# First FFN of a two-layer diffusion backbone: sums of modulation vectors as trees of accumulating DMAs, and both halves of a column block swept together in two PSUM banks

## The chip, the cores and the metric

The kernel runs on one core of one Trainium2 chip. The metric is the time of one execution in microseconds (us) on the device. The engines are TensorE (PE; PEld is its weight load), VectorE (DVE), ScalarE (ACT), GpSimd (POOL) and SyncE (SP), which here only issues DMAs. Each engine works through its own queue in order.

## The reference

Two layers run over 256 latent tokens, and the first layer also over 256 context tokens, with a model width of 1024 and an FFN width of 2816. Every sub-layer is modulated by vectors that come from a conditioning vector:

```
m  = (silu(c)     @ ada_w[i] + ada_b[i])     # 9 vectors of 1024 for latent tokens
mc = (silu(c_ctx) @ ada_w[i] + ada_b[i])     # the same for context tokens
x  = half_step_ffn(x,   m[0], m[1], m[2],  ffn_w_in[i, 0], ffn_w_out[i, 0], ...)
ctx = half_step_ffn(ctx, mc[0], mc[1], mc[2], ...)          # first layer only
# mixer with m[3..5] (layer 0: neighbourhood attention; layer 1: short convolution)
# second FFN with m[6..8]
# h = x * (1 + scale) + shift
# FFN: (silu(h @ w_in[:, :2816]) * (h @ w_in[:, 2816:])) @ w_out
# update: layer_norm(alpha * x + w * gate * y)
```

The modulation vectors need no token, only `ada_w`: 9 x 1024 columns by 1024 rows for each layer, 37.7 MB each. The two vectors that the first FFN itself starts with (m[0], m[1] and mc[0], mc[1]) are made ahead of it; the vectors spoken of here are the later ones.

## The kernel before

**Precision.** Most matrix products are made of three matmuls: each operand is split into a high part (ScalarE, `activation` Copy into a reduced-precision type, line 216) and a low part (VectorE, subtraction, line 219), and high x high, low x high and high x low are added in PSUM. A *unit* of weights is a tile of 128 x 1024 with one raw, one high and one low buffer. Raw buffers number four, high and low buffers five each; in the first FFN one further high and low buffer (`ext[0] = 1`, tags whx and wlx) takes one unit in six.

**The first FFN** (from line 597, loops from line 778) handles 512 tokens together. Its 22 column blocks of 128 come in three parts of 8, 8 and 6. A block has two halves, the SiLU half and the factor half, each a PSUM bank of 128 x 512 that is summed over eight K chunks of 128 rows. Column blocks go in panels of mostly two, which share four weight units. For each block after the first panel the loop sweeps over K for the first half, then over K for the second. `f0_mm` issues the matmuls (line 729), `f0_gate` (lines 738, 739, 118, 119) makes SiLU on ScalarE, the product on VectorE and the split. After each part `out_gemm` multiplies by the part's rows of `w_out` in two column halves of four token tiles each (lines 170 to 173), and `residual` adds the result times the gate to x. The gates are loaded from a table in DRAM (line 793) after the first part's column blocks. After the third part each token tile is normalized: `finish_stats` computes rs with two instructions on POOL (lines 435, 436), VectorE normalizes x (line 446), and TensorE transposes the result (hT, line 454).

**The background.** `tick()` is called after every six matmuls and advances a generator, `stream`, at a rate of 0.45 steps per tick, later 0.44, and 0.6 from the third group on. It runs `ada(vecs)` for seven groups of two vectors. Groups one to three each make a latent and a context vector from the same eight loads (m = 2, 3, 4 of layer 0); groups four to seven make two latent vectors from sixteen loads (m = 5, 6; m = 7, 8; then m = 0, 1 and m = 2, 3 of layer 1). One step loads 128 rows of `ada_w` (tag ar, three buffers; line 316, SP queue) and lets VectorE multiply them by a column of silu(c) and add them to a sum tile of 128 x 1024 (tag acc, two buffers; the first product is line 305, the others line 307; two instructions per vector and step). After the last load the sum over the 128 partitions is left. It is made on TensorE: two matmuls per vector with a matrix of ones (line 342, eight instructions per group in the trace), VectorE adds the bias row (line 343), and SP stores the row into `scr`, the table of modulation vectors in DRAM (line 345). Three steps pass between. A group has 12 steps with eight loads and 20 with sixteen.

In a later stage (`on_pool[0]` true, second FFN of layer 0 and beyond) the same function leaves the partition sum to `sum_up`: POOL reduces over partitions (line 356) and adds the row to the table with an accumulating DMA (line 357). For that the table's part for layer 1, vectors 4 to 8, is set to the bias beforehand (line 1162).

**What sets the order.** TensorE's instructions stand in program order. Those of the other engines are ordered by a planner that takes what is ready by priority, program order being the default; `tc.high_priority` moves work up (the unit splits by 40 instructions, the evacuation of output banks by 60 and more), and the background's last groups down by 20. On each queue the order so found is then fixed.

Of the kernel before, what the change touches and what calls it, by code (L numbers as in the profile page):

```python
# [10 lines left out]
F32 = mybir.dt.float32  # L11
# [7 lines left out]
P = 128  # L19
D = 1024  # L20
# [55 lines left out]
def backbone_kernel(  # L76
# [21 lines left out]
    ext = [1, 0]  # L98
# [183 lines left out]
    bias_rows = []  # L282
# [4 lines left out]
    def ada(vecs):  # L287
# [4 lines left out]
        def accumulate(l, m, k, w):  # L292
            with ExitStack() as st:
                for i in gate_ins + (last_lo if on_pool[0] else []):
                    st.enter_context(tc.issue_after(i.ins))
                for i, vec in enumerate(vecs):
                    if vec[:2] != (l, m):
                        continue
                    if k == 0:
                        acc[i] = hp.tile([P, D], F32, tag="acc", bufs=2, name=nm("acc"))  # L300
                    sc = cst[:, k, vec[2]:vec[2] + 1]
                    for h in range(2):
                        src, a = (c[:, h * 512:(h + 1) * 512] for c in (w, acc[i]))
                        if k == 0:
                            nc.vector.tensor_scalar(a, src, sc, None, op0=ALU.mult)
                        else:
                            nc.vector.scalar_tensor_tensor(out=a, in0=src, scalar=sc, in1=a,  # L307
                                                           op0=ALU.mult, op1=ALU.add)
            if on_pool[0] and k == KC - 1:
                sums.extend((vec, acc[i]) for i, vec in enumerate(vecs) if vec[:2] == (l, m))  # L310

        loaded = []
        for l, m in dict.fromkeys((l, m) for l, m, _ in vecs):
            for k in range(KC):
                w = hp.tile([P, D], F32, tag="ar", bufs=3, name=nm("ar"))
                sync.dma_start(w, ada_w[l, k * P:(k + 1) * P, m * D:(m + 1) * D])
                loaded.append((l, m, k, w))
                if len(loaded) > (ADA_LAG if gate_ins else 0):
                    accumulate(*loaded.pop(0))
                yield 1  # L320
# [6 lines left out]
        n = 2 * len(vecs)  # L327
        if not bias_rows:
            bias_rows.append(hp.tile([P, 512], F32, tag="adab", name=nm("adab")))
            nc.gpsimd.memset(bias_rows[0], 0.0)  # L330
        bt = bias_rows[0]
        for i, (l, m, v) in enumerate(vecs):
            sync.dma_start(bt[64 * i:64 * i + 64:32], ada_b[l, m * D:(m + 1) * D].rearrange("(a b) -> a b", b=512))
        yield 1
        yield 1
        yield 1
        rows = hp.tile([P, 512], F32, tag="adar", name=nm("adar"))
# [5 lines left out]
        nc.vector.tensor_tensor(out=rows[:32 * n], in0=ps[:32 * n], in1=bt[:32 * n], op=ALU.add)  # L343
# [254 lines left out]
    ab0 = hp.tile([P, D], F32, tag="acc", bufs=2, name="ab0")  # L598
# [14 lines left out]
    def start_tile():  # L613
# [3 lines left out]
        return hp.tile([P, D], F32, tag="ar", bufs=3, name=nm("ar"))  # L617
# [133 lines left out]
    for q, (k0, n) in enumerate(steps):  # L751
# [11 lines left out]
        run(nxt)  # L763
    sync.dma_start(win_sb, win_mask)
# [397 lines left out]
    sync.dma_start(scr[1][0, 4 * D:9 * D].rearrange("(a b) -> a b", a=16), ada_b[1, 4 * D:9 * D].rearrange("(a b) -> a b", a=16))  # L1162
# [131 lines left out]
```

## Time and profile before

| | |
|---|---|
| median of 3 runs | 1246.97 us (1245.27 to 1247.7) |
| the profiled execution | 1245.72 us, its span 1243.9 us |
| granted TensorE clock | 0.998 |
| first FFN | from the start to about 397 us |
| DMA packets | 275.67 MB, mean 222 GB/s |

The span runs from the first to the last instruction of the profiled execution; what lies around it makes its time 1.8 us longer. A profile row of a group gives line, engine, operation, output <- inputs, shapes and count, then busy time and the mean of one in ns, then the idle time of that engine just ahead of the group and what ended it. In the rows of stretches each engine's busy us are followed by its number of instructions, and the last three numbers are the granted clock, the busy share of the 16 DMA engines and the rate. The duration of a matmul row (about 390 ns) is its passage through the array; matmuls overlap, so the distance of their starts tells what one costs.

### The profile page before, as it was taken

To read this page: it belongs to the slowest core of one execution; us is meant where nothing else is said; L and a number is where in the kernel's file an instruction comes from. 1 tells how busy PE (TensorE), PEld (TensorE's weight loads), DVE (VectorE), ACT (ScalarE), POOL (GpSimd) and SP (SyncE) were. 2 spreads that over 40 slices of the span, in tenths; PEclk is the share of its full clock that TensorE was granted. 3 is DMA by queue.
4 is the path that set the end of the run, shared out by engine and by line. 5 is a ranking of instruction groups with operands and counts; after the bars stand their busy time and mean duration, and the time that the engine had idled before them with its cause. 6 is when DMAs were issued, how large, how long until landed. Compare 5 with 4: busy or idle time off the path is not lost.

```text
span 1243.9 us, 17235 instructions
## 1 busy us (share of the span) xinstructions
PE 1227.4 (99%) x5794; PEld 996.5 (80%) x5794; DVE 962.4 (77%) x1675; ACT 645.3 (52%) x1233; POOL 83.7 (7%) x93
## 2 busy tenths in 40 slices
PE   8999999999999999999999999999999999999997
PEld 6787778778778878777788888888878887888886
DVE  3698997888778866888877677878767798877646
ACT  2433132321325556587777635678535644677631
POOL 0000000000001111120000020020020110000200
PEclk9999999999999999999999999999999999999999
DMA  9876578778852654554899857889966764899741
GB/s 317 289 248 224 186 237 286 268 254 283 279 189 70 187 112 89 122 110 139 262 300 304 275 195 251 233 272 321 282 199 227 234 207 152 231 293 265 249 154 68
DMA packets 232304, 275.67 MB, mean 222 GB/s; under 512 B 59622, under 2 KB 178910, under 8 KB 232216
## 3 DMA queue, kind: packets, MB, share of 16 engines
q1 hardware_dynamic: 232020, 274.54, 71.9%
q8 instruction: 45, 0.74, 0.2%
q14 instruction: 43, 0.35, 0.1%
q0 software_dynamic: 160, 0.02, 0.0%
q10 hardware_dynamic: 36, 0.02, 0.0%
HBM read 265.27 MB, written 2.20 MB: 215 GB/s over the span
## 4 chain that ended last, share of the span: by engine, by line
PE 90%; DVE 5%; ACT 3%; DMA 1%; issue 1%; POOL 0%; SPq 0%; DVEq 0%; ACTq 0%
PE f L729 19%; PE w L170 17%; PE w L171 17%; PE w L173 17%; PE wkv L170 2%; PE wkv L171 2%; PE wkv L173 2%; PE wc L170 2%; PE wc L173 2%; PE wc L171 2%; PE ada L658 1%; PE S L1024 1%; PE hT L454 1%; DVE w1l L219 1%; PE wq L170 1%
## 5 line engine op out<-in xcount | busy, mean ns | idle before, releaser
L219 DVE TENSOR_TENSOR w1l<-w1r,w1h 128x512 fp32r<-128x512 f32 (+1 forms) x352 | 229.7, 697 | 44.0 <-ACT w1h L216 43.0
L216 ACT ACTIVATE w1h<-w1r 128x512 fp32r<-128x512 f32 (+1 forms) x352 | 198.7, 618 | 114.7 <-DMA w1r<-in_ffn_w_in_dram 38.3
L170 PE MATMUL w<-w1h,hTh 128*128 128x512 f32 x528 | 206.3, 391 | 1.2 <-ACT hTh L118 1.2
L171 PE MATMUL w<-w1l,hTh 128*128 128x512 f32 x528 | 205.6, 389 | 0.0
L307 DVE SCALAR_TENSOR_TENSOR acc<-ar,cst,acc 128x512 f32<-128x512 f32 x266 | 186.7, 749 | 14.4 <-DMA ar<-in_ada_w_dram 13.8
L170 PE MATMUL w<-w2h,gh 128*128 128x512 f32 (+1 forms) x446 | 173.3, 389 | 0.0
L171 PE MATMUL w<-w2l,gh 128*128 128x512 f32 (+1 forms) x446 | 172.3, 387 | 0.8 <-DVE w2l L219 0.8
L216 ACT ACTIVATE w2h<-w2r 128x512 fp32r<-128x512 f32 x176 | 101.5, 624 | 136.8 <-PE w L173 104.8
L173 PE MATMUL w<-w1h,hTl 128*128 128x512 f32 x528 | 162.7, 389 | 0.0
L219 DVE TENSOR_TENSOR w2l<-w2r,w2h 128x512 fp32r<-128x512 f32 x176 | 114.0, 688 | 56.0 <-ACT w2h L216 54.6
L173 PE MATMUL w<-w2h,gl 128*128 128x512 f32 (+1 forms) x446 | 136.1, 386 | 0.0
L729 PE MATMUL f<-h0h,w1h 128*128 128x512 f32 x352 | 133.8, 396 | 0.4 <-DVE h0h L684 0.4
L729 PE MATMUL f<-h0l,w1h 128*128 128x512 f32 x352 | 133.2, 391 | 0.0
L729 PE MATMUL f<-h0h,w1l 128*128 128x512 f32 x352 | 132.8, 390 | 0.0
L170 PEld LDWEIGHTS w<-w1h,hTh 128*128 128x128 f32 x528 | 99.1, 188 | 22.5 <-ACT hTh L118 2.1
L173 PEld LDWEIGHTS w<-w1h,hTl 128*128 128x128 f32 x528 | 99.0, 188 | 21.0 <-DVE hTl L119 0.4
L171 PEld LDWEIGHTS w<-w1l,hTh 128*128 128x128 f32 x528 | 99.1, 188 | 20.6 <-DVE w1l L219 0.3
L170 PEld LDWEIGHTS w<-w2h,gh 128*128 128x128 f32 x446 | 83.8, 188 | 19.2 <-issue 1.7
L171 PEld LDWEIGHTS w<-w2l,gh 128*128 128x128 f32 x446 | 83.8, 188 | 18.1 <-DVE w2l L219 1.7
L173 PEld LDWEIGHTS w<-w2h,gl 128*128 128x128 f32 x446 | 83.3, 188 | 17.1
L729 PEld LDWEIGHTS f<-h0h,w1h 128*128 128x128 f32 x352 | 66.3, 190 | 18.9 <-issue 4.2
L729 PEld LDWEIGHTS f<-h0l,w1h 128*128 128x128 f32 x352 | 65.5, 188 | 14.4 <-issue 0.6
(197 smaller groups left out, 1769.9 us busy)
## 6 DMA issues: line engine op xcount, KB each, us to landing
w1r<-in_ffn_w_in_dram SPq DMA_DIRECT2D x340, 256.0 KB
ar<-in_ada_w_dram SPq DMA_DIRECT2D x128, 512.0 KB
w2r<-in_ffn_w_out_dram SPq DMA_DIRECT2D x88, 512.0 KB
ar<-in_ada_w_dram SPq DMA_DIRECT2D x32, 256.0 KB
wkvr<-in_na_w_qkv_dram SPq DMA_DIRECT2D x32, 256.0 KB
wcr<-in_sc_w_in_dram SPq DMA_DIRECT2D x32, 256.0 KB
wqr<-in_na_w_qkv_dram SPq DMA_DIRECT2D x8, 512.0 KB
wor<-in_na_w_out_dram SPq DMA_DIRECT2D x8, 512.0 KB
```

What stands on the lines that cost most here:

```text
L170: nc.tensor.matmul(ps, lh, rh, start=first and i == 0, stop=False)
L171: nc.tensor.matmul(ps, lh, rl, start=False, stop=False)
L173: nc.tensor.matmul(ps, ll, rh, start=False, stop=last and i == n - 1)
L216: last_split[:] = [nc.scalar.activation(hi[:, a:a + m // W_HI], raw[:, a:a + m // W_HI], AF.Copy)]
L219: last_lo[:] = [nc.vector.tensor_tensor(out=lo[:, a:b], in0=raw[:, a:b], in1=hi[:, a:b].bitcast(F32), op=ALU.subtract)]
L307: nc.vector.scalar_tensor_tensor(out=a, in0=src, scalar=sc, in1=a, op0=ALU.mult, op1=ALU.add)
L454: nc.tensor.transpose(ps[:, k * P:(k + 1) * P], z[h][:, k * P:(k + 1) * P], ident)
L658: nc.tensor.matmul(ps[o:o + 32, 0:m], cst[:, a * kt + i, :], w[:, i, j, :], start=(a == 0 and i < 2), stop=(a == last and i >= kt - 2))
L729: nc.tensor.matmul(ps, w, hT0[k][part == 1], start=(k == part == 0), stop=(k == KC - 1 and part == 1))
L1024: nc.tensor.matmul(banks[i], (qh, qh, ql)[f][ps, qs], (kh, kl, kh)[f][ps, :], start=f == 0, stop=f == 2)
```

## The change

- In groups two to seven the partition sum is no longer on TensorE. When a vector's last product is issued, POOL's queue gets seven DMAs, each of which adds the upper half of the remaining rows of the sum tile to the lower half on chip (64 rows, 32, ... 1), and an eighth that adds the one row left to the table in DRAM. Each waits for the one before it. Two vectors that are ready together alternate.
- The first group is still summed on TensorE, without the bias; VectorE copies the result, and POOL adds it to the table.
- The bias is put into the whole of the table by three DMAs on SP at the beginning of the first FFN's main loop; the loads of bias rows and the later initialization go away.
- In the first FFN, sums have four buffers for two, and ada loads four for three; VectorE's products always run one step behind the load. The extra high and low weight buffer goes away. A group has 11 steps with eight loads and 19 with sixteen.
- Both banks of a column block are opened together, and one sweep over K alternates between them every six matmuls.

```diff
-    ext = [1, 0]
+    ext = [0, 0]
...
-    bias_rows = []
...
                     if k == 0:
-                        acc[i] = hp.tile([P, D], F32, tag="acc", bufs=2, name=nm("acc"))
+                        acc[i] = hp.tile([P, D], F32, tag="acc", bufs=2 if on_pool[0] else 4, name=nm("acc"))
...
-            if on_pool[0] and k == KC - 1:
-                sums.extend((vec, acc[i]) for i, vec in enumerate(vecs) if vec[:2] == (l, m))
+            if k == KC - 1:
+                ready = [(vec, acc[i]) for i, vec in enumerate(vecs) if vec[:2] == (l, m)]
+                if on_pool[0]:
+                    sums.extend(ready)
+                elif made[0]:
+                    n = P // 2
+                    while n:
+                        for _, a in ready:
+                            nc.gpsimd.dma_start(a[0:n], a[n:2 * n], accum_op=ALU.add)
+                        n //= 2
+                    for (l, m, v), a in ready:
+                        nc.gpsimd.dma_start(scr[l][v:v + 1, m * D:(m + 1) * D], a[0:1], accum_op=ALU.add)
...
-                w = hp.tile([P, D], F32, tag="ar", bufs=3, name=nm("ar"))
+                w = hp.tile([P, D], F32, tag="ar", bufs=3 if on_pool[0] else 4, name=nm("ar"))
...
-                if len(loaded) > (ADA_LAG if gate_ins else 0):
+                if len(loaded) > ADA_LAG:
                     accumulate(*loaded.pop(0))
...
-        for i, (l, m, v) in enumerate(vecs):
-            sync.dma_start(bt[64 * i:64 * i + 64:32], ada_b[l, m * D:(m + 1) * D].rearrange("(a b) -> a b", b=512))
-        yield 1
-        yield 1
-        yield 1
-        rows = hp.tile([P, 512], F32, tag="adar", name=nm("adar"))
+        for _ in range(3 if made[0] else 2):
+            yield 1
+        if made[0]:
+            return
+        rows = sp.tile([P, 512], F32, tag="s2", bufs=S2, name=nm("adar"))
...
-        nc.vector.tensor_tensor(out=rows[:32 * n], in0=ps[:32 * n], in1=bt[:32 * n], op=ALU.add)
+        nc.vector.tensor_copy(rows, ps)
         for i, (l, m, v) in enumerate(vecs):
-            sync.dma_start(scr[l][v, m * D:(m + 1) * D].rearrange("(a b) -> a b", b=512),
-                           rows[64 * i:64 * i + 64:32, :])
+            nc.gpsimd.dma_start(scr[l][v, m * D:(m + 1) * D].rearrange("(a b) -> a b", b=512),
+                                rows[64 * i:64 * i + 64:32, :], accum_op=ALU.add)
...
+    for l, v, r in ((0, 0, slice(2 * D, 9 * D)), (0, 1, slice(2 * D, 5 * D)), (1, 0, slice(0, 9 * D))):
+        sync.dma_start(scr[l][v, r].rearrange("(a b) -> a b", a=16), ada_b[l, r].rearrange("(a b) -> a b", a=16))
     sync.dma_start(win_sb, win_mask)
...
-                    bk = []
-                    for z in range(2):
-                        bk.append(mmb("f0", z))
-                        for k in range(0, KC, 2):
+                    bk = [mmb("f0", z) for z in range(2)]
+                    for k in range(0, KC, 2):
+                        for z in range(2):
                             f0_mm(bk[z], p, units, j, z, (k, k + 1))
                             tick()
...
-    sync.dma_start(scr[1][0, 4 * D:9 * D].rearrange("(a b) -> a b", a=16), ada_b[1, 4 * D:9 * D].rearrange("(a b) -> a b", a=16))
```

More of the change, by code (lines that the diff above doesn't have):

```diff
@@ L326, in ada @@
             return
[L327 to L331, printed above, removed]
-        for i, (l, m, v) in enumerate(vecs):
-            sync.dma_start(bt[64 * i:64 * i + 64:32], ada_b[l, m * D:(m + 1) * D].rearrange("(a b) -> a b", b=512))
-        yield 1
-        yield 1
-        yield 1
-        rows = hp.tile([P, 512], F32, tag="adar", name=nm("adar"))
+        for _ in range(3 if made[0] else 2):
[3 more added lines that the diff above has]
+        rows = sp.tile([P, 512], F32, tag="s2", bufs=S2, name=nm("adar"))
         ps = tpb("ada")
@@ L597, in backbone_kernel @@
     w_in, w_out = ffn_w_in[0, 0], ffn_w_out[0, 0]
-    ab0 = hp.tile([P, D], F32, tag="acc", bufs=2, name="ab0")
+    ab0 = hp.tile([P, D], F32, tag="acc", bufs=2 if on_pool[0] else 4, name="ab0")
     nc.vector.memset(ab0, 0.0)
@@ L616, in start_tile @@
             return hp.tile([P, 2, 512], F32, tag="pt", bufs=4, name=nm("ar")).rearrange("p a b -> p (a b)")
-        return hp.tile([P, D], F32, tag="ar", bufs=3, name=nm("ar"))
+        return hp.tile([P, D], F32, tag="ar", bufs=4, name=nm("ar"))
     marks = []
```

## The prediction

> **What bounds the kernel now.** I read the page first, then the busy time by stretches, then the chain of waits in order of time, then the timelines of single engines.
>
> ```profile
> PE 1227.4 (99%) x5794; PEld 996.5 (80%) x5794; DVE 962.4 (77%) x1675; ACT 645.3 (52%) x1233; POOL 83.7 (7%) x93
> ```
>
> ```profile
> core 0: us, PE busy (x) PEld busy (x) DVE busy (x) ACT busy (x) POOL busy (x), PEclk, DMA share, GB/s
> 97.00:135.00 38.00, 38.00 (x174) 30.48 (x170) 35.06 (x57) 10.59 (x19) 0.00 (x0) 1.00 0.65 222
> 135.00:173.00 38.00, 38.00 (x174) 30.49 (x170) 36.73 (x60) 9.20 (x16) 0.00 (x0) 1.00 0.63 200
> ...
> 268.00:314.00 46.00, 46.00 (x210) 37.24 (x206) 39.20 (x63) 12.11 (x22) 0.00 (x0) 1.00 0.80 265
> 314.00:361.00 47.00, 47.00 (x212) 38.21 (x204) 38.20 (x61) 15.86 (x28) 0.00 (x0) 1.00 0.74 246
> ```
>
> TensorE has the whole of these stretches of the first FFN, at a granted clock of 1.00. So time leaves this stage only with work that leaves TensorE, and every wait that reaches TensorE is added in full. VectorE comes next: 35.1 and 36.7 of 38 us while the second and third group of sums run. POOL does nothing here, so what is put on it has the engine to itself until the LayerNorm at the stage's end.
>
> The part that the change removes from TensorE shows in the chain of waits, once for each of the seven groups:
>
> ```profile
> 96.85 1.00 PE ada L342 x8
> ...
> 134.80 1.00 PE ada L342 x8
> ...
> 172.75 0.99 PE ada L342 x8
> ...
> 221.57 1.00 PE ada L342 x8
> ...
> 267.68 0.99 PE ada L342 x8
> ...
> 313.79 1.00 PE ada L342 x8
> ...
> 361.25 1.00 PE ada L342 x8
> ```
>
> **What leaves TensorE.** The timeline of PE around the first of them gives the price:
>
> ```profile
> 96.24 0.39 PE L729 MATMUL f<-h0h,w1l 128*128 128x512 f32 x1
> 96.47 0.39 PE L729 MATMUL f<-h0l,w1h 128*128 128x512 f32 x1
> 96.78 1.06 PE L342 MATMUL ada<-acc,ones 128*32 128x512 f32 x8
> 97.78 0.50 PE L729 MATMUL f<-h0h,w1h 128*128 128x512 f32 x1
> 98.12 0.39 PE L729 MATMUL f<-h0h,w1l 128*128 128x512 f32 x1
> ```
>
> Ordinary matmuls start 0.227 us apart (96.24 to 96.47 is 0.23). From 96.47 to 98.12 two periods should pass, 0.45 us; 1.65 pass. One group costs TensorE 1.20 us: the chain's 1.00 and 0.2 of switching around it. Six groups of seven go to DMAs: 6 x 1.20 = 7.2 us. The first stays as it is.
>
> **The two-bank sweep.** It issues the same matmuls, so TensorE gains nothing by itself. What it moves is when a weight buffer comes free. One unit is two pieces on ACT and two on VectorE:
>
> ```profile
> L216 ACT ACTIVATE w2h<-w2r 128x512 fp32r<-128x512 f32 x176 | 101.5, 624 | 136.8 <-PE w L173 104.8 <-DMA w1r<-in_ffn_w_in_dram 15.5 <-DMA w2r<-in_ffn_w_out_dram 8.1
> L219 DVE TENSOR_TENSOR w2l<-w2r,w2h 128x512 fp32r<-128x512 f32 x176 | 114.0, 688 | 56.0 <-ACT w2h L216 54.6
> ```
>
> That is 2 x 0.624 + 2 x 0.688 = 2.6 us. A panel of two column blocks holds four units; the ring had five and one extra buffer, and loses the extra one. Before, the third unit of the next panel takes the buffer that the last sweep frees 18 matmuls before its end, and is needed 12 matmuls into the next: 30 x 0.227 = 6.8 us. Now the second unit takes the one freed 36 matmuls before the end and is needed 12 in: 48 x 0.227 = 10.9 us. So with one buffer less the column blocks are safer than before. The output matmuls keep their order and only lose the buffer: between their two column halves the second unit has 18 + 6 matmuls, 5.4 us, for 2.6 us of work. With VectorE as full as above this can reach TensorE. Bounds: nothing, or the whole 2.6 us at each of three places, 7.8 us; I take 0.5, since 2.8 us are left over. SiLU now finds its bank done six matmuls (1.4 us) before the other instead of 24. The last gate is needed 12 to 18 matmuls after the last sweep: I take nothing, at most 0.4 us three times.
>
> **VectorE.** Rows of its groups in 97 to 173 us:
>
> ```profile
> L307 DVE SCALAR_TENSOR_TENSOR acc<-ar,cst,acc 128x512 f32<-128x512 f32 x56 | 38.6, 751 | 0.0
> L305 DVE TENSOR_SCALAR acc<-ar,cst 128x512 f32<-128x512 f32 x8 | 3.5, 481 | 2.9 <-PE ada L342 2.9
> L343 DVE TENSOR_TENSOR adar<-ada,adab 128x512 f32<-128x512 f32 x2 | 1.4, 684 | 0.0
> ```
>
> A later group takes fewer background steps, 11 for 12 and 19 for 20, so the same sums come faster. Groups two and three had 24 steps in 76 us; 22 take (76 - 2.4) x 22/24 = 67.5. VectorE's 71.8 us are 42.1 of sums, 1.4 of L343 and 28.3 that go with the matmuls, which become 25.1. 42.1 + 25.1 = 67.2 of 67.5: full. Its waits for L342 go, and with a lag of one step and a fourth buffer also those for the loads. A backlog would be worked off in the fourth group, where the rate falls. Between 0 and 3 us on TensorE; I take 0.5.
>
> **POOL and the trees.** Each vector becomes seven halvings and one DMA into the table in DRAM, eight DMAs that must wait for each other, all on POOL's queue. The trace has no halving. Nearest are the DMAs that POOL already accumulates with, and one small load into on-chip memory:
>
> ```profile
> L357 POOL DMA_DIRECT2D scr<-red x5: 997/997/1118, 727.2 to 1156.2; - x5
> ...
> DMA to landing us min/median/max: 2.7/3.4/4.9
> ```
>
> ```profile
> 1.37 2.21 DMA crow<-in_c_ctx_dram
> ```
>
> ```profile
> L255 ACTq DMA_DIRECT2D crow<-in_c_ctx_dram x1: 289/289/289, 1.4 to 1.4; - x1
> ```
>
> The small load needs 2.21 - 0.29 = 1.9 us after its issue; behind POOL's 1.0 that makes 2.9. A halving lies between 2.7 and 3.4 us; I take 2.8, by the lower end, because it ends on chip as that load does and the first FFN has the DMA engines 0.63 to 0.80 busy. The halvings also move 127 rows of 4 KB, 0.52 MB; at the 380 GB/s of the row below, 1.4 us if nothing overlaps. A tree: 7 x 2.8 + 3.4 + 1.4 = 24.4 us; with the ends, 7 x 2.7 + 2.7 + 0 = 21.6 to 8 x 3.4 + 1.4 = 28.6.
>
> ```profile
> 60.00:65.00 5.00, 5.00 (x24) 4.14 (x23) 5.00 (x9) 2.14 (x5) 0.00 (x0) 1.00 1.07 380
> ```
>
> How often do trees come? Groups two and three make two at once, 33.6 us apart: these fit. From the fourth on each group makes two, one after each eight loads, in 19 steps of (361.25 - 172.75)/80 = 2.36 less the 1.2 saved per group, about 2.3: 43.7 us, one tree per 21.9. At 24.4 they fall behind, 2.5 us each. The first of these eight is ready at about 182 us (group four starts at 173, 9.5 us earlier by three saved steps and 2.4 by TensorE, and needs nine steps). Four sum buffers let a sum start while three older trees are still at work, so VectorE isn't held up. But POOL's queue is in order, and behind the trees stands the LayerNorm:
>
> ```profile
> 385.71 0.19 POOL L435 TENSOR_TENSOR rs<-mv,lnc 128x1 f32<-128x1 f32 x1 [381.47 <-DVE mv L433]
> 385.98 0.57 POOL L436 TENSOR_TENSOR rs<-rs,lnc 128x1 f32<-128x1 f32 x1
> ```
>
> ```profile
> 388.58 0.87 PE hT L454 x8
> ```
>
> rs is wanted at 385.7 - 7.2 = 378.5, and the transposes on TensorE follow 2.9 us after it, with the normalizing of x in between and no slack that I can see. POOL is free when the eighth tree has issued its last DMA, 2.4 us before the tree ends: 182 + 8T - 2.4 <= 378.5 gives T <= 24.9 us. My 24.4 fits, barely. Each us of T above it costs TensorE 8 us.
>
> One rule of the skill speaks against putting this on POOL. The VectorE products of L305 take 481 ns where L307 takes 751 for the same shape, so they run in a faster mode; two of them fall in each tree. The Trainium skill, SBUF — State Buffer, section "SBUF: two separate sides", says that while VectorE runs an instruction in a two-port mode GpSimd cannot write the descriptors of its DMAs. By that rule a tree could grow by up to 2 x 0.48 = 1.0 us and the end by 8; as L305 has 1.0 of every 21.9 us, 0.1 per tree is likelier, and no run yet shows it. The same skill, DMA: Bandwidth & Descriptors, section "Anatomy of one DMA — SWDGE (gpsimd) path", gives 2.0 us per DMA plus bytes at 436 GB/s: a tree of 17.2 us, an estimate by that page, with nothing late. The rows above say more per DMA, and I go by them.
>
> **The rest.** Twenty-eight small DMAs leave SP's queue (fourteen bias rows, fourteen stores) and three initializing ones join it ahead of the mask, rope and ada loads; TensorE waited for none of them: nothing. The one of the later stage moves here. The first group's store goes over POOL and lands 3.4 us after its issue; the gate load waits for it on SP with ada and w2 loads behind it. One saved step (38.0/12 = 3.2 us) covers nearly all of that, and the residual that reads the gate comes after the whole first quarter of the output matmuls: nothing. The trees read twice and write once, 12 x 0.52 x 3 = 18.7 MB over 270 us, 69 GB/s beside 265: below the 380 seen, so nothing (bound 2 us).
>
> **Sum.** 7.2 - 0.5 - 0.5 = 6.2 us. The profiled execution took 1245.7 us (span 1243.9): 1239.5. It lies 1.3 below the median of 1247.0, from which the sum gives 1240.8. I forecast 1240.0.
>
> **Rivals.** *POOL falls behind (slower).* The place is rs L435 behind the eighth tree; it decides from T = 24.9 us, 2.9 us a halving. For it: the median landing of 3.4, and T within 0.5 us of the limit by my own count. Against it: those landings end in DRAM. At 28.6 us rs is 30 us late, 1239.5 + 30 = 1269; in the middle, 26.7, 15 us late, 1254. *The gain is eaten.* VectorE is full in groups two and three and the output matmuls lose their spare buffer: 3 us of backlog and 2 to 4 of refills leave 1243 to 1246. For it: 67.2 of 67.5. Against it: the load waits on VectorE end, and the sweeps relieve it.
>
> **How the numbers follow.** Forecast 0.60, by itself 1237 to 1243. POOL behind 0.27, eaten 0.13. A measurement of this kernel can tell 0.2%, 2.5 us, from no change. Faster: 0.60, the part of the second with T up to 25.4 (0.03) and the mildest of the third (0.04): 0.67. Same: 0.09 of the third and 0.02 of the second, 0.11. Slower 0.22. The range begins at 1237, the forecast without its two stalls (1239) less the 2 us by which runs of this kernel differ, and ends at 1257, T = 27; about 0.1 lies above, 0.05 below.
>
> **What would show it.** No L342 after the first; starts of TensorE 0.227 us apart through the stage, transposes hT at about 382. POOL's DMAs: the gap from one halving to the next should be 2.7 to 3.0 us. If rs stands behind a DMA of the last tree, or VectorE waits on a sum buffer, T was too small in my count. If w L171 waits on w2l at the middle of an output matmul, the buffer was missed.

## The result: slower by 2.1 %, and the profile after

The changed kernel takes 1273.32 us (median of four, 1273.07 to 1273.72) beside 1247.05 (1245.27 to 1247.7) for the one before: a ratio of 1.0213, 95 % interval 1.0201 to 1.0225. The forecast was 1240.0, its range ended at 1257. The profiled execution took 1273.07 us, its span is 1271.0 (before 1243.9).

The page of the changed kernel: the span, engines, DMA queues and chain.

```profile
span 1271.0 us, 17247 instructions
...
PE 1232.7 (97%) x5746; PEld 1001.0 (79%) x5746; DVE 959.2 (75%) x1669; ACT 643.7 (51%) x1233; POOL 161.1 (13%) x190
...
q0 software_dynamic: 4064, 6.33, 3.4%
...
PE 65%; DMA 15%; DVE 9%; issue 5%; ACT 3%; POOL 2%; SPq 0%; DVEq 0%; POOLq 0%; ACTq 0%
```

TensorE issues 48 matmuls fewer (5746 for 5794), as meant. POOL's queue moves 4064 packets, and DMAs hold 15 % of the chain that ended last. The same kernel in stretches of the first FFN's middle:

```profile
core 0: us, PE busy (x) PEld busy (x) DVE busy (x) ACT busy (x) POOL busy (x), PEclk, DMA share, GB/s
97.00:135.00 38.00, 38.00 (x169) 31.48 (x168) 38.00 (x62) 10.46 (x19) 6.20 (x8) 1.00 0.86 268
...
200.00:250.00 50.00, 47.12 (x200) 38.08 (x199) 39.23 (x63) 12.91 (x24) 12.89 (x16) 0.97 0.97 323
250.00:300.00 50.00, 42.65 (x164) 32.42 (x163) 44.09 (x70) 10.51 (x19) 11.62 (x14) 0.90 0.95 293
...
314.00:361.00 47.00, 45.84 (x190) 37.73 (x191) 28.05 (x45) 13.71 (x24) 14.62 (x19) 0.93 0.65 178
```

TensorE no longer has the whole of the stage: it is idle for 2.9 and 7.4 of 50 us, and the granted clock falls to 0.90 there. The DMA engines, 0.80 busy before, are 0.95 to 0.97 busy from 200 to 300 us, and 0.65 busy after 314 (before 0.74). So the background's products ran *earlier* than before, not later: the last starts at 330.1 us, before at 352.2.

Where the 27.1 us of span come from shows in the starts of rs on POOL. The first is at 403.76 (before 385.71, forecast 378.5): 18.0 us are lost up to that point, and the forecast's gain with them. 3.9 more are lost up to the second layer norm (609.10 for 587.19), 0.8 from there to the last rs and 4.4 after it. From 97 to 350 us TensorE is idle for 13.9 us; much of the rest of the loss is matmuls that start further apart, as the rows below show.

POOL's timeline at the end of the trees, and the landings of its DMAs (output <- input, size, median us from issue to landing):

```profile
386.79 0.78 POOL L319 DMA_DIRECT2D scr<-acc  x1 [1.68 <-DMA acc<-acc]
403.76 0.19 POOL L438 TENSOR_TENSOR rs<-mv,lnc 128x1 f32<-128x1 f32 x1 [16.19 <-DVE mv L436]
```

```profile
acc<-acc POOLq DMA_DIRECT2D x12, 256.0 KB, 7.0
acc<-acc POOLq DMA_DIRECT2D x12, 128.0 KB, 5.8
acc<-acc POOLq DMA_DIRECT2D x12, 64.0 KB, 4.6
acc<-acc POOLq DMA_DIRECT2D x12, 32.0 KB, 4.9
acc<-acc POOLq DMA_DIRECT2D x12, 16.0 KB, 4.0
acc<-acc POOLq DMA_DIRECT2D x12, 8.0 KB, 4.2
acc<-acc POOLq DMA_DIRECT2D x12, 4.0 KB, 4.6
scr<-acc POOLq DMA_DIRECT2D x12, 4.0 KB, 3.3
```

The landings of a tree add up to 38.4 us, where 24.4 were forecast. Yet the place that the slower rival named isn't where it hurts: ahead of rs POOL was idle for 16.19 us and waited for VectorE's mv. The loss reaches TensorE by another way, which two of the stalls show. ScalarE, VectorE and TensorE of the changed kernel, around 206 us:

```profile
192.47 0.58 ACT L741 ACTIVATE sil<-f 128x512 f32<-128x512 f32 x1
204.96 0.64 ACT L118 ACTIVATE gh<-sil 128x512 fp32r<-128x512 f32 x1 [11.91 <-DVE sil L742]
205.50 3.21 ACT L216 ACTIVATE w1h<-w1r 128x512 fp32r<-128x512 f32 x6
```

```profile
196.59 1.41 DVE L306 SCALAR_TENSOR_TENSOR acc<-ar,cst,acc 128x512 f32<-128x512 f32 x2 [2.23 <-DMA ar<-in_ada_w_dram]
199.09 1.41 DVE L306 SCALAR_TENSOR_TENSOR acc<-ar,cst,acc 128x512 f32<-128x512 f32 x2 [1.08 <-DMA ar<-in_ada_w_dram]
201.22 1.42 DVE L306 SCALAR_TENSOR_TENSOR acc<-ar,cst,acc 128x512 f32<-128x512 f32 x2 [0.71 <-DMA ar<-in_ada_w_dram]
...
204.24 0.68 DVE L742 TENSOR_TENSOR sil<-sil,f 128x512 f32<-128x512 f32 x1
...
208.20 1.29 DVE L219 TENSOR_TENSOR w1l<-w1r,w1h 128x512 fp32r<-128x512 f32 x2
```

```profile
206.16 0.50 PE L732 MATMUL f<-h0h,w1h 128*128 128x512 f32 x1
208.94 0.80 PE L732 MATMUL f<-h0h,w1l 128*128 128x512 f32 x1 [2.28 <-DVE w1l L219]
209.53 0.63 PE L732 MATMUL f<-h0l,w1h 128*128 128x512 f32 x1
209.96 0.63 PE L732 MATMUL f<-h0h,w1h 128*128 128x512 f32 x1
210.39 0.63 PE L732 MATMUL f<-h0h,w1l 128*128 128x512 f32 x1
```

Read it backwards. TensorE waits 2.28 us for w1l. VectorE makes w1l late because ScalarE made w1h late (six splits stand at 205.50 behind gh), and because more products of the background stand ahead of w1l. gh waits 11.91 us for the gate's product L742, though SiLU was done at 193.05. L742 stands in VectorE's queue behind the background's products, which wait 4.0 us for ada loads that are late and take most of the other time themselves. Behind the stall the matmuls start 0.43 us apart for a while instead of 0.23. The largest group of stalls, 6.4 us in four waits at the second output matmul (253 to 267 us), came the same way: there L742 stood behind 6.8 us of late loads, and gh waited 13.22 us for it.

The second stall shows a held sum buffer. VectorE and TensorE around 312 us:

```profile
309.77 0.88 DVE L304 TENSOR_SCALAR acc<-ar,cst 128x512 f32<-128x512 f32 x2 [2.89 <-DMA scr<-acc]
310.57 2.07 DVE L306 SCALAR_TENSOR_TENSOR acc<-ar,cst,acc 128x512 f32<-128x512 f32 x3
...
314.42 1.29 DVE L219 TENSOR_TENSOR w1l<-w1r,w1h 128x512 fp32r<-128x512 f32 x2
```

```profile
315.16 0.79 PE L732 MATMUL f<-h0h,w1l 128*128 128x512 f32 x1 [3.26 <-DVE w1l L219]
```

ScalarE had made the high parts by 310.2. VectorE stood 2.89 us until a tree's last DMA had landed, did products and residuals that stand ahead in its queue, and made the low part 3.26 us too late.

VectorE's waits in the background's products over the whole kernel, changed and then before; they all lie between 97 and 380 us:

```profile
L306 DVE SCALAR_TENSOR_TENSOR acc<-ar,cst,acc 128x512 f32<-128x512 f32 x266 | 186.2, 741 | 31.5 <-DMA ar<-in_ada_w_dram 31.2
...
L307 DVE SCALAR_TENSOR_TENSOR acc<-ar,cst,acc 128x512 f32<-128x512 f32 x266 | 186.7, 749 | 14.4 <-DMA ar<-in_ada_w_dram 13.8
```

So VectorE's waits for ada loads in these products add up to 31.2 us (before 13.8), those for a sum buffer to 4.6, and gh waits 75.4 us for the product between 97 and 380 us (before 53.6).

### The profile page after: what moved, and what is told of

Same layout as the page of the kernel before. It is cut to its first block, busy times and chain, and to the rows that moved or that the text cites. A ratio compares the mean times of both kernels' runs of the same rounds, so it can differ in the third digit from the quotient of the medians.

```text
span 1271.0 us, 17247 instructions
## 1 busy us (share of the span) xinstructions
PE 1232.7 (97%) x5746; PEld 1001.0 (79%) x5746; DVE 959.2 (75%) x1669; ACT 643.7 (51%) x1233; POOL 161.1 (13%) x190
## 3 DMA queue, kind: packets, MB, share of 16 engines
q0 software_dynamic: 4064, 6.33, 3.4%
## 4 chain that ended last, share of the span: by engine, by line
PE 65%; DMA 15%; DVE 9%; issue 5%; ACT 3%; POOL 2%; SPq 0%; DVEq 0%; POOLq 0%; ACTq 0%
PE w L171 14%; PE w L170 14%; PE w L173 14%; DMA acc<-acc 12%; PE f L732 7%; PE wkv L170 2%; PE wkv L171 2%; PE wkv L173 2%; PE wc L170 2%; PE wc L173 2%; PE wc L171 2%; DMA ar<-in_ada_w_dram 1%; DVE acc L306 1%; DVE w1l L219 1%; ACT pr L1036 1%
## 5 line engine op out<-in xcount | busy, mean ns | idle before, releaser
L219 DVE TENSOR_TENSOR w1l<-w1r,w1h 128x512 fp32r<-128x512 f32 (+1 forms) x352 | 231.0, 699 | 41.1 <-ACT w1h L216 39.2
L306 DVE SCALAR_TENSOR_TENSOR acc<-ar,cst,acc 128x512 f32<-128x512 f32 x266 | 186.2, 741 | 31.5 <-DMA ar<-in_ada_w_dram 31.2
L171 PE MATMUL w<-w1l,hTh 128*128 128x512 f32 x528 | 205.6, 389 | 0.0
L171 PE MATMUL w<-w2l,gh 128*128 128x512 f32 (+1 forms) x446 | 174.8, 393 | 3.3 <-DVE w2l L219 3.2
L170 PEld LDWEIGHTS w<-w1h,hTh 128*128 128x128 f32 x528 | 99.2, 188 | 22.6 <-ACT hTh L118 2.1
L171 PEld LDWEIGHTS w<-w1l,hTh 128*128 128x128 f32 x528 | 99.2, 188 | 20.3
L171 PEld LDWEIGHTS w<-w2l,gh 128*128 128x128 f32 x446 | 84.8, 190 | 23.6 <-DVE w2l L219 7.1
L316 POOL DMA_DIRECT2D acc<-acc x84 | 68.5, 858 | 201.1 <-DMA acc<-acc 180.4
L732 PEld LDWEIGHTS f<-h0h,w1l 128*128 128x128 f32 x352 | 66.9, 191 | 21.9 <-DVE w1l L219 8.1
```

Source lines behind the costliest of these rows:

```text
L170: nc.tensor.matmul(ps, lh, rh, start=first and i == 0, stop=False)
L171: nc.tensor.matmul(ps, lh, rl, start=False, stop=False)
L219: last_lo[:] = [nc.vector.tensor_tensor(out=lo[:, a:b], in0=raw[:, a:b], in1=hi[:, a:b].bitcast(F32), op=ALU.subtract)]
L316: nc.gpsimd.dma_start(a[0:n], a[n:2 * n], accum_op=ALU.add)
L732: nc.tensor.matmul(ps, w, hT0[k][part == 1], start=(k == part == 0), stop=(k == KC - 1 and part == 1))
```

## The experiments

Each measured time is a median, and in brackets stands the ratio to the kernel before, run beside it, with its 95 % interval. In the expectations of no_halvings, thin_halvings and sweep_no_extra, A is the theory that the halvings cost the time (A1 by their bytes, A2 by the long chain that holds the sum buffers), and B that the lost weight buffer, the joint sweep or the faster steps do.

### What the halvings cost, and by what

**no_halvings.** The halvings are left out.

```diff
-                    n = P // 2
-                    while n:
-                        for _, a in ready:
-                            nc.gpsimd.dma_start(a[0:n], a[n:2 * n], accum_op=ALU.add)
-                        n //= 2
```

> The changed kernel without its seven halvings per vector: row 0 of each sum tile alone is added to the table, so the modulation vectors of groups two to seven are incomplete; all other work and its order stay. Theory A (the halvings are at fault, by the load that they put on the DMA engines or by the time that they hold buffers): 1239 to 1244 us, the 6 us gain that was forecast, no idle TensorE between 180 and 330 us. Theory B (the halvings are harmless; the thinner weight ring, the joint sweep or the faster steps starve TensorE): 1262 us or more.

Measured: 1249.7 us (1.0021, 1.0011 to 1.003). So the halvings cost 23.6 us, but without them the kernel is still not faster than before: the time lies between the ranges of A and B. The starts on POOL in this run say how often sums are ready when no tree holds them: the fifth at 174.39, the twelfth at 307.73, one per 19.0 us, not 21.9. In the changed kernel the trees of the same vectors issue their last DMA from 228.45 to 386.79, one per 22.6. The trees can't keep up: the last reaches its eighth DMA 79 us after the last sum is ready where nothing holds it. Two things are not the halvings' doing, since this run has them too: from 200 to 250 us the DMA engines are 0.91 busy at 323 GB/s, and VectorE waits 19.0 us for banks that TensorE has not finished (18.1 in the change, 0.3 before).

**thin_halvings.** Every halving moves 16 of the 1024 columns.

```diff
-                            nc.gpsimd.dma_start(a[0:n], a[n:2 * n], accum_op=ALU.add)
+                            nc.gpsimd.dma_start(a[0:n, 0:16], a[n:2 * n, 0:16], accum_op=ALU.add)
```

> As the changed kernel, but each halving adds only 16 of the 1024 columns (the rest of the sum is left out): as many DMAs in as long a chain of waits on POOL's queue, 1/64 of the bytes. If the bytes are the cost (A1: the DMA engines are full, ada loads land late, VectorE waits in order): 1239 to 1246 us, steps of the tree of 2 to 3.5 us. If the number of chained DMAs is the cost (A2: 84 issues, each landing 4 to 5 us later, hold the sum buffers): trees still above 30 us and 1258 us or more. B: 1262 or more.

Measured: 1278.13 us (1.0244, 1.0223 to 1.0265). A 64th of the bytes costs no less. The landings are still 3.0 to 4.4 us for a halving, 28.5 us for a tree. VectorE and TensorE of this run, at the second output matmul:

```profile
247.51 1.28 DVE L219 TENSOR_TENSOR w2l<-w2r,w2h 128x512 fp32r<-128x512 f32 x2
259.45 0.88 DVE L304 TENSOR_SCALAR acc<-ar,cst 128x512 f32<-128x512 f32 x2 [10.66 <-DMA scr<-acc]
260.25 0.68 DVE L742 TENSOR_TENSOR sil<-sil,f 128x512 f32<-128x512 f32 x1
```

```profile
261.65 0.80 PE L170 MATMUL w<-w2h,gh 128*128 128x512 f32 x1 [12.57 <-ACT gh L118]
```

Here the whole way is in four rows: VectorE wants to begin a sum, all four buffers are held by trees, it stands for 10.66 us until a tree's last DMA lands, the gate's product stands behind it, and TensorE loses 12.57 us. VectorE waits 21.5 us for buffers in this run, and 13.1 for ada loads, 34.6 together as against 35.8 in the change (4.6 and 31.2). Whether the missing bytes let the loads come sooner, or VectorE, held elsewhere, met them later, these rows don't tell.

**three_halvings.** The four smaller halvings are left out.

```diff
-                    while n:
+                    while n >= 16:
```

> Only the halvings to 64, 32 and 16 rows are made; the four smaller ones are left out, so each sum lacks most of its rows. By the landings of the changed kernel a tree is 7.0 + 5.8 + 4.6 + 3.3 = 20.7 us, under the 21.9 us in which a sum is made, and 7/8 of the halvings' bytes still move. Theory (the number of chained DMAs per tree, which hold sum buffers and with them VectorE): near the kernel without halvings (1249.7), 1249 to 1256. Rival (the halvings' bytes, which make ada and w loads late): most of the 23.6 us stay, 1266 to 1271.

Measured: 1258.13 us (1.0094, 1.0078 to 1.0109), between the two. Four DMAs fewer per tree, with 7/8 of the bytes left, take away 15 of the 23.6 us (4 of them at the kernel's very end, see the last section); 8 stay. VectorE has no wait for a sum buffer left and still waits 27.9 us for ada loads, so the sum of the waits for loads alone does not set the time.

**five_sums.** Five sum buffers and three ada buffers for four and four.

```diff
-                        acc[i] = hp.tile([P, D], F32, tag="acc", bufs=2 if on_pool[0] else 4, name=nm("acc"))
+                        acc[i] = hp.tile([P, D], F32, tag="acc", bufs=2 if on_pool[0] else 5, name=nm("acc"))
...
-                w = hp.tile([P, D], F32, tag="ar", bufs=3 if on_pool[0] else 4, name=nm("ar"))
+                w = hp.tile([P, D], F32, tag="ar", bufs=3, name=nm("ar"))
```

> The changed kernel, all computed, with five sum buffers and three ada buffers for four and four. Theory (trees hold sum buffers; with three of them VectorE waited 26.5 us for one, with four 4.6): VectorE's wait for a sum buffer goes to 0, but it is small already, and one ada buffer less lets loads come later: 1268 to 1276. Rival (the sum buffers are the whole cost): 1250 to 1262.

Measured: 1276.61 us (1.0235, 1.0214 to 1.0255). The wait for a sum buffer is gone, those for ada loads are 39.2 + 8.1 us. One wait takes the other's place. As an ada buffer went too, this doesn't price the buffers alone.

### The sweep and the weight buffer

**one_bank.** The changed kernel with the old order of the sweep: the second bank is opened after the first is swept.

```diff
-                    bk = [mmb("f0", z) for z in range(2)]
-                    for k in range(0, KC, 2):
-                        for z in range(2):
+                    bk = []
+                    for z in range(2):
+                        bk.append(mmb("f0", z))
+                        for k in range(0, KC, 2):
```

> The changed kernel with the old order of matmuls: one half of a column block swept over K after the other; the rest as changed. If the joint sweep is part of the harm (SiLU and the product come late, ScalarE waits for the gate's product with weight pieces queued behind): 1255 to 1265 us. If it protects, as the prediction counted (10.9 against 6.8 us for a unit): 1280 us or more. If it doesn't matter: 1271 to 1276.

Measured: 1275.05 us (1.0224, 1.0207 to 1.0241). The sweep's order does not matter to the loss.

**sweep_no_extra.** The kernel before with the joint sweep (the change's lines) and `ext = [0, 0]`, nothing else.

> The kernel before with the joint sweep and without the extra weight buffer, its sums on TensorE as before: what this half of the change does alone. The prediction's count (safer column blocks, thinner output matmuls) gives 1247 to 1249 us. Theory B gives 1255 us or more. Theory A has nothing against 1247.

Measured: 1249.56 us (1.0029, 1.0018 to 1.0041).

**before_no_extra.** The kernel before without that buffer, with the old sweep.

```diff
-    ext = [1, 0]
+    ext = [0, 0]
```

> The kernel before with the extra high and low weight buffer taken away (ext = [0, 0]) and nothing else. Theory (the handover from the first FFN to the mixer lives on that buffer): 1249 to 1251, with TensorE waiting for wql and kTl between 400 and 460 us. Rival (the joint sweep causes those waits): 1246 to 1248.

Measured: 1251.82 us (1.0043, 1.0031 to 1.0056). So it is the lost buffer that costs, not the sweep. The first rs is 1.8 us late in this run, the fifth (second layer norm) 7.4: most of it is lost in between, in the handover to the mixer, where TensorE has no wait of the kind before. TensorE of this run:

```profile
406.19 0.50 PE L171 MATMUL wq<-wql,hTh 128*128 128x512 f32 x1 [1.33 <-DVE wql L219]
442.23 0.49 PE L1024 MATMUL S<-kTl,qTh 64*128 64x512 f32 x2 [1.84 <-DVE kTl L119]
```

The changed kernel has the same two, 1.32 and 1.72 us, at 422.43 and 458.33. This is also why no_halvings isn't faster: its first rs is 2.6 us earlier than before's, its fifth 3.8 later.

### What the sums on TensorE were worth

**sums_left_out.** The kernel before, where groups two to seven make no partition sum.

```diff
+        if made[0]:
+            for i, (l, m, v) in enumerate(vecs):
+                sync.dma_start(scr[l][v, m * D:(m + 1) * D].rearrange("(a b) -> a b", b=512),
+                               bt[64 * i:64 * i + 64:32, :])
+            yield 1
+            return
         rows = hp.tile([P, 512], F32, tag="adar", name=nm("adar"))
```

> The kernel before, in which groups two to seven leave out the partition sum: no matmul with ones and no addition of the bias; the store writes the bias row alone, so the modulation is wrong from there on. It prices the term 7.2 us. Theory: TensorE's share leaves in full, 1239 to 1241. Rival (VectorE or the loads set the pace as soon as the sums are gone): 1243 to 1247.

Measured: 1250.55 us (1.0031, 1.0021 to 1.0042). The 48 matmuls, 7.2 us of a busy TensorE, are gone, and the kernel is slower, above both ranges. By stretches:

```profile
200.00:250.00 50.00, 48.64 (x215) 39.95 (x214) 38.65 (x63) 16.46 (x30) 0.00 (x0) 1.00 0.87 296
250.00:300.00 50.00, 47.27 (x198) 37.69 (x197) 42.78 (x69) 9.85 (x17) 0.00 (x0) 0.97 0.84 277
300.00:350.00 50.00, 47.89 (x205) 39.17 (x204) 36.87 (x59) 14.03 (x25) 0.00 (x0) 0.97 0.73 239
```

TensorE is idle for 6.2 us where it had been full, and the clock falls. The last product is at 338.5 us; before it was at 352.2.

**no_halvings_slow, slow_steps.** The background's rate from the fourth group on (it is set when three groups are made) is lower, in the kernel without halvings and in the changed one.

```diff
-ADA_SLOW, ADA_FAST, ADA_SLOWEST = 3, 0.6, 0.13
+ADA_SLOW, ADA_FAST, ADA_SLOWEST = 3, 0.48, 0.13
```

> The kernel without halvings (1249.7; the sums lack all rows but the first) at 0.48 steps per tick for 0.6. Without halvings the last product stood at 306 us, before at 352; at 0.48 it should stand near 345. Theory (rate): the stall at 250 to 300 us goes, with what the clock loses behind it, and the handover's 6 us stay: 1244 to 1247. Rival (the stall has nothing to do with the rate): 1249 to 1251.

> The changed kernel with 0.48 background steps per tick from the fourth group on, for 0.6; nothing else. Theory (the groups came too fast: loads, trees and weights together ask for more than the DMA engines move, and the trees fall behind the sums): the stalls of TensorE after 200 us shrink to a few us and the handover's 6 us stay, 1251 to 1262. Rival (a tree holds up VectorE at any rate, or the trees now end after the LayerNorm is due): 1268 or more.

Measured: 1248.47 us (1.0012, 1.0002 to 1.0023) and 1273.55 (1.0214, 1.0196 to 1.0233). The theory of the rate falls, and in an instructive way: without halvings the last products are at 306.2 us with 0.48 and at 306.0 with 0.6, in the changed kernel at 329.5 and 329.4. In these kernels, with the sums off TensorE, the tick's rate, between these two values, doesn't set the place of the background.

**sums_paced.** sums_left_out with two tiny matmuls per group at the old place in TensorE's order.

```diff
+            ps = tpb("ada")
+            for i in range(len(vecs)):
+                nc.tensor.matmul(ps[32 * i:32 * i + 32, 0:8], ones, acc[i][:, 0:8], start=True, stop=True)
```

> The kernel before without the sums of groups two to seven (1250.6), with two tiny matmuls of 128 x 8 per group in their place on TensorE, whose results nobody reads. They cost TensorE some 0.3 us a group, 2 us in all. Theory (the sums' matmuls, which free the two sum buffers at a fixed place in TensorE's order, paced the background; without them the sums run ahead, the last product at 338 us for 352, and loads and VectorE crowd the weights): the stalls at 200 to 350 us go, the last product is back near 347, 1240 to 1243. Rival (the pace has nothing to do with it): 1248 to 1251, faster than which it can't be by two more matmuls.

Measured: 1244.78 us (0.9985, 0.9977 to 0.9994). Matmuls whose results nobody reads make the kernel 5.7 us faster (0.46 % between the two ratios), 1.8 us short of the theory's range. The last product is back at 351.6 us, and by stretches:

```profile
200.00:250.00 50.00, 49.33 (x219) 39.95 (x218) 38.60 (x61) 17.28 (x30) 0.00 (x0) 1.00 0.81 276
250.00:300.00 50.00, 48.60 (x217) 39.54 (x216) 40.51 (x66) 10.91 (x19) 0.00 (x0) 1.00 0.79 258
300.00:350.00 50.00, 50.00 (x225) 41.14 (x224) 41.56 (x66) 14.42 (x25) 0.00 (x0) 1.00 0.87 293
```

The stalls shrink from 6.2 to 2.1 us, and the clock stays. So the sums' matmuls had a second office. Their place in TensorE's order paced loads and products; that they did it by freeing the two sum buffers fits, as the tiny matmuls read the same sums. With the work gone and the pace kept, the gain is 1.9 us (0.15 %), not 7.2.

**no_halvings_paced, after_paced.** The same idea in the changed kernel: one tiny matmul per group reads the group's last ada tile.

```diff
         if made[0]:
+            ps = tpb("ada")
+            nc.tensor.matmul(ps[0:32, 0:8], ones, w[:, 0:8], start=True, stop=True)
             return
```

> The changed kernel without halvings (1249.7; sums lack all rows but the first), with one tiny matmul of 128 x 8 per group that reads the last ada tile of the group, so that TensorE's order frees that buffer. Theory (lost pace): the last product comes later than 306 us, near 340; the stall at 250 to 300 us goes and the handover's 6 us stay, 1245 to 1248. Rival: 1249 to 1251.

> The changed kernel, all computed, with one tiny matmul per group that reads the last ada tile of the group. Theory (lost pace and the trees' length each take a part): better than the change by the part that the crowd costs, 1256 to 1268; the trees and the handover still cost what they cost. Rival (only the trees' length counts): 1271 to 1276.

Measured: 1254.13 us (1.0056, 1.0037 to 1.0075) and 1277.43 (1.0241, 1.0216 to 1.0266). Both lie above the ranges of theory and rival. It paced only in part: the last product of the first came at 319.3 (306.0 without), not near 340, that of the second at 338.9, and the stall at 250 to 300 stayed (46.66 of 50 us). That four buffers of each kind make the hold too loose is a guess. So pace isn't shown to be a part of the changed kernel's loss; it isn't excluded either.

**patient, no_halvings_patient.** A product is planned only after the ada load two further on has been issued, in the changed kernel and without halvings.

```diff
-ADA_LAG = 1
+ADA_LAG = 2
...
             with ExitStack() as st:
+                if not on_pool[0]:
+                    st.enter_context(tc.issue_after(newest[0].ins))
...
-                sync.dma_start(w, ada_w[l, k * P:(k + 1) * P, m * D:(m + 1) * D])
+                newest[:] = [sync.dma_start(w, ada_w[l, k * P:(k + 1) * P, m * D:(m + 1) * D])]
```

> The changed kernel, all computed, in which a group's product is planned only after the ada load two further on has been issued (one later than in the change), so that a late load finds no VectorE waiting for it. Theory (VectorE stands in its queue for late ada loads, 31.2 us in the change, with SiLU's product behind them, then gh, then the weight splits, then TensorE): those waits fall below 20 us and the time to 1255 to 1268. Rival (the sum buffers held by the trees take their place, as they did with thin halvings, 21.5 us): 1270 to 1280.

> The same in the kernel without halvings (1249.7; the sums lack all rows but the first). There the last SiLU product ahead of the second output matmul stood 5.5 us behind products of the background, and TensorE lost 2 us to it and some more to the clock. Theory (the background's products stand ahead of the gate): the stall goes or shrinks, 1244 to 1248. Rival: 1249 to 1252.

Measured: 1280.93 us (1.0271, 1.0258 to 1.0284) and 1253.75 (1.0044, 1.0028 to 1.0061). Missed, above both ranges: in the first VectorE waits 29.1 us for ada loads as it did.

### Versions that might have beaten both

**slow_extra, no_halvings_slow_extra.** The slower rate, the weight buffer back, three sum and three ada buffers, with and without halvings.

```diff
-ADA_SLOW, ADA_FAST, ADA_SLOWEST = 3, 0.6, 0.13
+ADA_SLOW, ADA_FAST, ADA_SLOWEST = 3, 0.48, 0.13
...
-    ext = [0, 0]
+    ext = [1, 0]
...
-                        acc[i] = hp.tile([P, D], F32, tag="acc", bufs=2 if on_pool[0] else 4, name=nm("acc"))
+                        acc[i] = hp.tile([P, D], F32, tag="acc", bufs=2 if on_pool[0] else 3, name=nm("acc"))
```

> The changed kernel at 0.48 steps per tick, and with the extra high and low weight buffer of the kernel before (ext = [1, 0]), which is paid for with one sum buffer and one ada buffer (three each). The full computation. Theory (rate and weight buffer are what the change lost): 1241 to 1250. Rival (three sum buffers are too few for trees of some 38 us, VectorE stands): 1255 to 1275.

> The same as the one with the slower steps and the extra weight buffer, with the halvings left out (only the first row of each sum is added to the table). It shows what the six sums on TensorE are worth when neither the rate nor the weight buffer takes it back. Theory: 7.2 us under the kernel before, 1238 to 1242. Rival (something else stands against the gain): 1243 to 1248.

Measured: 1284.34 us (1.0299, 1.0285 to 1.0313) and 1247.14 (1.0001, 0.9992 to 1.001). The first is above both ranges: with three sum buffers VectorE waits 26.5 us for one. Without trees the handover's loss is gone, as the buffer is back, but a stall of 5.2 us at 256 (TensorE waits for gh) eats the rest.

**pool_sum.** One partition reduction on POOL for the seven halvings, with before's buffers.

```diff
+                        red = hp.tile([P, D], F32, tag="red", bufs=1, name=nm("red"))
+                        nc.gpsimd.partition_all_reduce(red, a, P, ReduceOp.add)
+                        nc.gpsimd.dma_start(scr[l][v:v + 1, m * D:(m + 1) * D], red[0:1], accum_op=ALU.add)
```

> The changed kernel with one partition reduction on POOL in place of the seven halvings, and with before's buffers (two sums, three ada loads, the extra weight buffer). A reduction takes about 6 us in the later stage; two are ready at once in groups two and three, 12 us. Theory (the long chain and the lost weight buffer cost what the sums gave): 1239 to 1244. Rival (two sum buffers held by POOL stop VectorE, or POOL's reduction slows it): 1247 to 1256.

Measured: 1280.64 us (1.0278, 1.0264 to 1.0292), far above both ranges. VectorE's and POOL's groups between 97 and 380 us:

```profile
L306 DVE SCALAR_TENSOR_TENSOR acc<-ar,cst,acc 128x512 f32<-128x512 f32 x168 | 130.5, 822 | 8.1 <-DMA ar<-in_ada_w_dram 8.0
L304 DVE TENSOR_SCALAR acc<-ar,cst 128x512 f32<-128x512 f32 x20 | 40.4, 2055 | 11.1 <-POOL red L315 7.0 <-DMA ar<-in_ada_w_dram 4.1
```

```profile
L315 POOL PARTITION_ALL_REDUCE red<-acc x12 | 75.3, 6278 | 188.4 <-DVE acc L306 182.7 <-DMA scr<-red 5.7
```

The first products of a sum take 2055 ns for 482, the others 822 for 749. On a VectorE that was full that is 20 x 1.57 + 168 x 0.073 = 44 us more. No version with all the work was faster than the kernel before.

## Why the prediction was wrong, point by point

- *6 x 1.20 = 7.2 us leave TensorE.* The matmuls left, the time didn't. Taken out alone they cost 3.9 us (0.31 %), with their pace kept they give 1.9. The prediction took it that time leaves with work that leaves TensorE, and then looked for waits only in what the change adds. That VectorE was full, and the DMA engines 0.80 busy, was in the rows; that the sums' place in TensorE's order held both back was not asked.
- *A tree, 24.4 us.* Mis-sized: 38.4 by the landings. The nearest rows (3.4 and 2.9 us) came from five DMAs of 4 KB in later stages and one small load at the start. Halvings of 256 to 4 KB landed in 7.0 to 4.0 us amid loads. The count also took trees one after another. They overlap: POOL issues DMAs of two trees in a row (two at 207.55), so one tree ends every 22.6 us, but each holds its sum buffer for the whole of its own landings or longer.
- *One tree per 21.9 us.* Wrong: 19.0 when nothing holds the sums. The sums' place on TensorE had set a part of the slower pace (last product at 352.2 us before, 338.5 without the sums, 306.0 in no_halvings, which also has the change's buffers and steps). Trees that end every 22.6 us fell behind by 3.6 us each, and the first of the eight had its last DMA 54 us after the time at which no_halvings has that sum ready.
- *"Four sum buffers let a sum start while three older trees are still at work, so VectorE isn't held up."* This is the step that failed, together with the statement that VectorE's waits for loads go. VectorE is held: in the change itself 4.6 us for sum buffers and 31.2 for loads (before 13.8), in thin_halvings up to 10.66 us at a time. Behind the held products stand the gate, which was priced at "nothing, at most 0.4 us three times", and the weight splits. The prediction named a wait of VectorE on a sum buffer as a sign that T was too small, but gave it no price.
- *Extra bytes: nothing, bound 2 us.* Not shown to be the cause: with a 64th of them the time doesn't fall (thin_halvings). Not shown to be nothing either: three_halvings keeps 7/8 of the bytes and 8 us of the loss, but also chained DMAs. The 380 GB/s held against them was a row with a DMA share above 1; the stage now runs at 323 with 0.97.
- *The weight buffer, 0.5 us at the output matmuls.* Wrong place: 5.4 us (0.43 %) when taken away alone, mostly at the handover to the mixer, which the prediction didn't look at. The sign that it named, w L171 waiting for w2l, does appear in the change (1.30 us at 258.06), but behind gh; in sweep_no_extra, also without the buffer, TensorE has no wait there.
- *The two-bank sweep: no gain by itself.* Right (one_bank, sweep_no_extra).
- *POOL behind, rs late behind the eighth tree.* The rival came nearest (1254 to 1269 for 1273.3) and had slow trees as the cause, but the wrong place: rs waited for VectorE. That its size was so near is in part luck.
- *The products of L305 against POOL's DMAs, 0.1 us a tree.* In the change (L304) they keep their 481 ns and an issue takes POOL about 0.8 us; no such effect shows here.

How the 20.6 us at the first rs (403.76 beside 383.13 without halvings) divide between held buffers and late loads stays open: in thin_halvings VectorE waits less for loads, in five_sums no more for buffers, and the time stayed. Shown is that the number of chained DMAs matters more than their bytes. Trees on two queues, or both vectors of a pair in one tree, weren't tried.

## What to carry to other kernels

Before taking work off the busiest engine, ask what else it does there: a step in a fixed order that frees a buffer can be a throttle, and when it goes, whatever it held back runs ahead into the engines and queues that had just enough room. A chain of DMAs must be sized by landings under the load of its own stage, and compared with the rate at which work comes when nothing holds it. Queues that are worked in order carried a late product of the background straight to the main path here, so look at what stands behind each new wait before counting buffers.

## What the runs showed of the hardware

- The time from issue to landing of a DMA that adds on chip depended little on its size: 3.0 to 4.4 us with rows of 64 bytes, 4.0 to 7.0 with whole rows, from 4 to 256 KB. The Trainium skill, DMA: Bandwidth & Descriptors, section "Anatomy of one DMA — SWDGE (gpsimd) path", gives 2.0 us plus the bytes at 436 GB/s, for 256 KB an estimate of 2.6 us by that page's figures; here 7.0 was measured, beside other transfers.
- Behind the stall of 2.28 us matmuls started 0.43 us apart until 211.7, and after one of 3.26 us until 320.9, 5.7 us long. So these two cost 1.4 and 2.8 us beyond their own length. Not every stall does: in the same kernel the starts behind the wait of 1.72 us at 458.33 are soon 0.23 us apart again. The Trainium skill, TensorE: Matmul & The Clock Gate, section "Part 1: The HAM clock gate", has 426.7 ns for a matmul of this width on a cold array, which agrees; it closes the gate after an idle window of about 3.4 us, and here a wait of 2.28 us already had this behind it.
- In pool_sum products of L304 are slow beside a reduction on POOL: two of them take 5.15 us from 197.89, with a reduction from 198.08 to 204.35, and 0.88 us in the change. The Trainium skill, SBUF — State Buffer, section "SBUF: two separate sides", describes a port pair of VectorE and GpSimd that one of them holds for a whole instruction. The rows fit that in part: the second product ends 1.3 us before the reduction does.
- Between the last rs and the end lie 10.4 to 10.5 us in every run with 84 halvings, 6.5 with three_halvings and 5.9 to 6.1 without any; the last store's issue ends at 1263.6 of 1271.0 in the change. What runs there the profile doesn't show. It is 4.4 of the change's 27 us.
